# Making part of the routing one-hots on GpSimd instead of VectorE in a two-layer decoder block

## The chip, the cores and the metric

The kernel runs on one core of a Trainium2 chip. The metric is the device time of one execution in microseconds. A core has five engines that run side by side, each through its own list of instructions in order: TensorE (PE in the profile, its weight loads PEld), VectorE (DVE), ScalarE (ACT), GpSimd (POOL) and SyncE (SP, which here only issues transfers). Semaphores hold an instruction until what it needs is there.

## The reference: a two-layer decoder with an expert mixer in each layer

512 tokens of width 1024 pass two layers, the first with gated linear attention, the second with sliding-window attention. Each layer ends in a mixer over 16,384 single-neuron experts (PEER). For a token, 8 heads pick 16 experts each, by two keys of 128 values: expert number = first key x 128 + second key. Cut to what matters:

```
v1, i1 = top_k(s1, 16);  v2, i2 = top_k(s2, 16)       # per head, 128 keys each
cs, ci = top_k(v1[:, None] + v2[None, :], 16)
e = i1[ci // 16] * 128 + i2[ci % 16]                  # the 16 experts of a head
g = softmax(cs)
a = gelu(x . u_tab[e])
y = sum over heads and experts of g * a * v_tab[e]
```

## The kernel before: tiles, stages and what sets the order

Of the 512 tokens, 128 are done by *gathers*: GpSimd fetches the rows of the chosen experts from memory (line 717), and VectorE multiplies and adds them one expert at a time (lines 725 and 735). These are spread thinly over the whole dense stage of the layer.

The other 384 tokens are done *densely*: every expert is computed for every token, and a weight of zero takes out those that were not chosen. The function `dense` does it, once per layer. Its work has two parts.

The first part, called *pass 1* in the first layer and *pass 2* in the second, makes the routing weights. The 384 tokens are taken in 24 groups of 16. For a group, `routed(g)` works out the 128x128 matrix of weights of each token as a product of one-hot matrices: 128 (head, choice) pairs lie on the partitions, and for each token there is a matrix `o1` whose row has a one in the column of the pair's first key, and a matrix `o2` with a one at the second key. `og` is `o2` times the weight g, as a high and a low f16 half. Two matmuls per token, `o1` transposed times each half of `og`, sum over the pairs and give the token's 128x128 matrix. On VectorE a group takes one compare for `o2` (line 577), one compare for `o1` (line 579) and two products for `og` (line 582), each over 128 x 2048 f16 numbers. Compares are between `iop`, the numbers 0 to 127, each twice, and `i1T` or `i2T`, the transposed keys. TensorE then does 32 matmuls (line 590, the *routing matmuls*), ScalarE copies them out of PSUM (line 591), and a transfer writes them to a buffer in memory (`wd`, line 592).

Beside each group stands one call of `act(i)`, for one of 128 tiles of 128 experts: it loads the tile, splits it into a high half (ScalarE, line 243) and a low half (VectorE, line 244), and does 24 matmuls with the hidden state (line 605, the *activation matmuls*). 28 such tiles are done ahead.

The second part goes over all 128 tiles: it reads the weights back in slots (line 611), multiplies them with the activations (line 627), and accumulates the outputs with `stage2` (line 639).

The buffers that matter: `o1` has two buffers, `o2` and `og` have one each, `wt` two. The order of instructions on every engine is set by the framework's scheduler at build time, which goes by priorities and its own estimates of durations; a change of the code can move instructions on engines that it does not touch. The gathers have the lowest priority; each gather needs one of four row buffers.

The keys reach `dense` by `route_block`: three transposes on TensorE (line 545), and copies on ScalarE to `i1T`, `i2T` and the weights' halves `ghl` for each of three blocks of 128 tokens.

Of the kernel before, what the change touches and what calls it, by code (L numbers as in the profile page):

```python
# [10 lines left out]
F32 = mybir.dt.float32  # L11
# [5 lines left out]
ALU = mybir.AluOpType  # L17
# [3 lines left out]
P = 128  # L21
# [16 lines left out]
NBD = 3  # L38
TG = 16
# [9 lines left out]
def kernel(ctx, tc, x, c_col, pos, mod_w, mod_b, norm_g, w_in, w_gl, w_g2, b_g2, gla_ng, gla_wo,  # L49
                      kv_mod_w, kv_mod_b, kv_ng, kv_w, swa_wq, sinks, swa_wo, peer_wq, subk, peer_u, peer_v,  # L50
                      u_t, v_t, fin_g, out):
    nc = tc.nc

    const = ctx.enter_context(tc.tile_pool(name="const", bufs=1))
    mid = ctx.enter_context(tc.tile_pool(name="mid", bufs=1))
# [35 lines left out]
    iop = const.tile([P, NK, 2], F16, tag="iop", name="iop")  # L91
# [13 lines left out]
    def ps_tile(env, kind):  # L105
        pool, tag, bufs = env.psum[kind]
        if not isinstance(tag, str):
            pool, tag, bufs = tag[env.turn % len(tag)]
            env.turn += 1
        return pool.tile([P, 512], F32, tag=tag, name=f"ps_{kind}", bufs=bufs)  # L110
# [408 lines left out]
    def route_front(env, l, hT, rp):  # L519
        v16 = rp.tile([P, 16, TOPK], F32, tag="v16", name="v16")  # L520
        i16 = rp.tile([P, 16, TOPK], U32, tag="i16", name="i16")
        wpool, wtag, _, wbufs = env.w
        for ch in range(4):
            pq = ps_tile(env, "mm")
            for q in range(4):
                w = wpool.tile([P, KT, P], F32, tag=wtag, name="w", bufs=wbufs)
                nc.sync.dma_start(w, peer_wq[l, ch * 4 + q])
                for kt in range(KT):
                    nc.tensor.matmul(pq[:, ts(q, P)], w[:, kt, :], hT[:, kt, :], start=kt == 0, stop=kt == KT - 1)  # L529
            qq = env.big.tile([P, 512], F32, tag=env.qq, name="qq")  # L530
            nc.scalar.copy(qq, pq)
            psc = ps_tile(env, "sc")
            for q in range(4):
                nc.tensor.matmul(psc[:, ts(q, P)], qq[:, ts(q, P)], sk_sb[l][:, q % 2, :], start=True, stop=True)
            sc = env.tmp.tile([P, 512], F32, tag=env.t2k, name="scg", bufs=env.scb)
            nc.scalar.copy(sc, psc)
            topk16(rp, [(sc[:, ts(q, P)], v16[:, ch * 4 + q, :], i16[:, ch * 4 + q, :]) for q in range(4)], NK)
        return route(rp, v16, i16)

    def route_block(env, l, b, hT, rp):  # L540
        g, i1, i2 = route_front(env, l, hT, rp)
        e = b - 1
        pt = ps_tile(env, "tr")
        for q, t in enumerate((i1, i2, g.rearrange("p h k -> p (h k)"))):
            nc.tensor.transpose(pt[:, ts(q, P)], t, ident)
        nc.scalar.copy(i1T[e], pt[:, 0:P])
        nc.scalar.copy(i2T[e], pt[:, P:2 * P])
        gT = rp.tile([P, P], F32, tag="gT", name="gT")
        nc.scalar.mul(gT, pt[:, 2 * P:3 * P], GSC)
        nc.scalar.copy(ghl[e][:, 0, :], gT)  # L550
        nc.vector.tensor_tensor(ghl[e][:, 1, :], gT, ghl[e][:, 0, :], op=ALU.subtract)

    def dense(l, yps):
# [5 lines left out]
        with tc.tile_pool(name="dna", bufs=1, reuse_waits="tile") as da, \  # L559
# [5 lines left out]
            def routed(g):  # L565

                e, s16 = g // 8, ts(g % 8, TG)
                i1, i2, gh = (t.rearrange("p (u w) -> p u w", w=2) for t in (
                    i1T[e][:, s16], i2T[e][:, s16], ghl[e][:, 0, s16]))
                gl = ghl[e][:, 1, s16].rearrange("p (u w) -> p u w", w=2)  # L570
                codes = iop.unsqueeze(1).to_broadcast([P, TG // 2, NK, 2])

                def wide(t):
                    return t.unsqueeze(2).to_broadcast([P, TG // 2, NK, 2])

                o2 = do_.tile([P, TG // 2, NK, 2], F16, tag="o2", name="o2")
                nc.vector.tensor_tensor(o2, codes, wide(i2), op=ALU.is_equal)
                o1 = do_.tile([P, TG // 2, NK, 2], F16, tag="o1", name="o1", bufs=2)
                nc.vector.tensor_tensor(o1, codes, wide(i1), op=ALU.is_equal)
                og = do_.tile([P, 2, TG // 2, NK, 2], F16, tag="og", name="og")  # L580
                for n, gn in enumerate((gh, gl)):
                    nc.vector.tensor_tensor(og[:, n], o2, wide(gn), op=ALU.mult)
                wt = do_.tile([P, NK, TG], F32, tag="wt", name="wt", bufs=2)
                for q in range(4):
                    i = 4 * g + q
                    pm = yps.tile([P, 4, NK], F32, tag=banks[i % (3 if g < 16 else 6)], name="pm")
                    for t in range(4):
                        for n in range(2):
                            u, w = 2 * q + t // 2, t % 2
                            nc.tensor.matmul(pm[:, t, :], o1[:, u, :, w], og[:, n, u, :, w], start=n == 0, stop=n == 1)  # L590
                    nc.scalar.copy(wt[:, :, ts(q, 4)], pm.rearrange("p t i -> p i t"))
                nc.sync.dma_start(wd[ts(g, P), :], wt.rearrange("p i t -> p (i t)"))
# [266 lines left out]
    def swa_d(Y, yctx, mod, Ak, Bk, A, B, A4, B4, rbase):  # L859
        with ExitStack() as stack, tc.tile_pool(name="sd", bufs=1, reuse_waits="tile") as sp, \  # L860
# [50 lines left out]
            def finish(b):  # L911
                for ch in range(2):
                    w = stream_w(env, swa_wo[ch])
                    py = ps_tile(env, "mm")
                    for kt in range(KT):
                        nc.tensor.matmul(py, oT[b - 1][:, kt, :], w(kt), start=kt == 0, stop=kt == KT - 1)  # L916
                    gated_add(env, XD[b - 1], ch, py, gate[:, ts(ch, 512)])
                nc.sync.dma_start(xs[b], XD[b - 1])
                hT = h4k("hTd")
                env.psum["tr"] = env.psum["m0"]  # L920
                peer_h(env, b, XD[b - 1], A4, B4, hT)
                with prio(rbase):
                    route_block(renv, 1, b, hT, sr)
# [29 lines left out]
    i1T = [mid.tile([P, P], F16, tag=f"i1T{b}", name="i1T") for b in range(NBD)]  # L953
    i2T = [mid.tile([P, P], F16, tag=f"i2T{b}", name="i2T") for b in range(NBD)]
    ghl = [mid.tile([P, 2, P], F16, tag=f"ghl{b}", name="ghl") for b in range(NBD)]
    hH = mid.tile([P, KT, TD], F32R, tag="hH", name="hH")
    hL = mid.tile([P, KT, TD], F32R, tag="hL", name="hL")
    a0 = mid.tile([P, NH * TOPK], F32, tag="a0", name="a0")
# [34 lines left out]
    def fin0(env, pool, b, xt):  # L993
        nc.sync.dma_start(xs[b], xt)
        hT = pool.tile([P, KT, P], F32, tag="hTd", name="hTd", bufs=2)
        renv = Env()
        renv.psum, renv.tmp, renv.t2k, renv.big, renv.qq, renv.w = env.rpsum, pool, "rsc", pool, "qq", (pool, "w", 2, 3)
        renv.scb = 4
        if b == 0:
            ht = gather_front(env, pool, 0, xt, hT, m0[:, 40:48], cols["A2"], m0[:, 24:32])  # L1000
            with prio(R0):
                gs.append((ht, *gather_sel(renv, 0, hT, pool)))
        else:
            peer_h(env, b, xt, cols["A2"], m0[:, 24:32], hT)
            with prio(R0):
                route_block(renv, 0, b, hT, pool)
# [123 lines left out]
```

## Time and profile before

| what | value |
|---|---|
| median of 3 runs | 3281.14 us (3279.89 to 3283.94) |
| the profiled execution | 3281.36 us, of which the span is 3279.7 us |
| TensorE busy | 3087.9 us, 94% |
| VectorE busy | 2396.3 us, 73% |
| ScalarE busy | 1282.9 us, 39% |
| GpSimd busy | 610.3 us, 19% |
| first to last routing matmul, pass 1 | 578.1 to 721.8 us |
| first to last routing matmul, pass 2 | 2171.4 to 2302.9 us |

Matmuls are pipelined and overlap in the record, so TensorE's rate is read from starts, not from durations. VectorE's instructions overlap a little too: one starts before the one ahead of it has ended. A bracket behind a row of the timeline tells how long the engine was idle before it and what ended that. A granted clock of 1.00 is 2.4 GHz.

### The profile page before, as it was taken

The numbers are of one execution on the slowest core, as the hardware profiler recorded it, in microseconds if no ns is written. First come the engines' busy times: TensorE is split into PE (matmuls) and PEld (weight loads), VectorE is DVE, ScalarE is ACT, GpSimd is POOL, SyncE is SP. The second block draws the span as 40 slices with busy tenths as digits, with TensorE's granted clock in tenths as the row PEclk, the third lists the DMA queues.
The fourth block names the chain that finished last, engine by engine and source line by source line (L and its number), as shares of the span: only waits on it lengthen the run. The fifth ranks groups of instructions, "written<-read, shape, count | busy, mean of one in ns | idle before, by whom it ended". The sixth has DMA issues, their size and how long they took to land.

```text
span 3279.7 us, 45577 instructions
## 1 busy us (share of the span) xinstructions
PE 3087.9 (94%) x16858; PEld 2633.6 (80%) x16858; DVE 2396.3 (73%) x4699; ACT 1282.9 (39%) x1991; POOL 610.3 (19%) x542
## 2 busy tenths in 40 slices
PE   6999985999999999999997889899899999999998
PEld 4765675998889999999876446899789999999997
DVE  7754699989777777777655344999877777777776
ACT  3422322653333333333662344256333333333333
POOL 0000000005333333333000000000433232223230
PEclk9989998999999999999998989999999999999999
DMA  7666675789889898898744225658998888888874
GB/s 238 229 243 237 237 261 169 261 283 345 307 311 317 291 321 311 301 322 287 239 143 145 84 77 193 213 200 294 329 343 311 300 278 305 276 302 303 272 265 154
DMA packets 264888, 844.44 MB, mean 257 GB/s; under 512 B 27844, under 2 KB 77380, under 8 KB 258520
## 3 DMA queue, kind: packets, MB, share of 16 engines
q1 hardware_dynamic: 190936, 573.06, 49.4%
q0 software_dynamic: 73728, 268.47, 24.3%
q8 instruction: 132, 2.16, 0.3%
q14 instruction: 92, 0.75, 0.1%
HBM read 784.27 MB, written 57.16 MB: 257 GB/s over the span
## 4 chain that ended last, share of the span: by engine, by line
PE 81%; DVE 10%; DMA 5%; ACT 2%; issue 1%; SPq 0%; DVEq 0%; ACTq 0%
PE pa L605 32%; PE Y L639 30%; PE ps_mm L529 3%; PE pm L590 3%; PE ps_m L902 2%; DMA v<-in_v_t 1%; PE ps_mm L435 1%; PE ps_mm L260 1%; PE ps_mm L261 1%; PE ps_mm L259 1%; PE ps_mm L916 1%; DMA w<-in_gla_wo 1%; PE ps_po L808 1%; DMA w<-in_mod_w 1%; DVE s L446 1%
## 5 line engine op out<-in xcount | busy, mean ns | idle before, releaser
L717 POOL DMA_INDIRECT gu<-in_peer_u,ei x256 | 314.8, 1230 | 1991.3 <-DVE gu L725 1192.1
L244 DVE TENSOR_TENSOR XL<-u,XH 128x1024 fp32r<-128x1024 f32 x256 | 313.2, 1224 | 351.7 <-PE pa L605 197.4
L639 PE MATMUL Y<-XH,WH 128*128 128x512 f32 x1536 | 480.4, 393 | 9.8 <-ACT WH L243 9.8
L639 PE MATMUL Y<-XH,WL 128*128 128x512 f32 x1536 | 478.5, 393 | 4.1 <-DVE WL L244 4.1
L639 PE MATMUL Y<-XL,WH 128*128 128x512 f32 x1536 | 478.5, 392 | 0.2
L243 ACT CAST XH<-u 128x1024 fp32r<-128x1024 f32 x256 | 269.1, 1052 | 432.1 <-PE pa L605 359.2
L605 PE MATMUL pa<-hH,XH 128*128 128x384 f32 x2048 | 412.4, 341 | 2.2 <-ACT XH L243 1.6
L243 ACT CAST XH<-v 128x1024 fp32r<-128x1024 f32 x256 | 268.8, 1050 | 363.4 <-PE Y L639 312.2
L605 PE MATMUL pa<-hL,XH 128*128 128x384 f32 x2048 | 404.9, 336 | 0.0
L717 POOL DMA_INDIRECT gu<-in_peer_v,ei x256 | 290.9, 1136 | 608.6 <-DVE yg L735 567.4
L605 PE MATMUL pa<-hH,XL 128*128 128x384 f32 x2048 | 401.5, 335 | 2.2 <-DVE XL L244 2.2
L244 DVE TENSOR_TENSOR XL<-v,XH 128x1024 fp32r<-128x1024 f32 x256 | 313.0, 1223 | 109.9 <-ACT XH L243 106.2
L605 PEld LDWEIGHTS pa<-hH,XH 128*128 128x128 f32 x2048 | 365.1, 188 | 20.4 <-ACT XH L243 1.8
L605 PEld LDWEIGHTS pa<-hH,XL 128*128 128x128 f32 x2048 | 358.2, 188 | 3.2 <-DVE XL L244 2.9
L605 PEld LDWEIGHTS pa<-hL,XH 128*128 128x128 f32 x2048 | 358.8, 188 | 1.6 <-issue 0.8
L639 PEld LDWEIGHTS Y<-XH,WL 128*128 128x128 f32 x1536 | 289.0, 188 | 67.4 <-DVE WL L244 5.4
L639 PEld LDWEIGHTS Y<-XL,WH 128*128 128x128 f32 x1536 | 289.0, 189 | 64.4 <-DVE XL L244 1.1
L639 PEld LDWEIGHTS Y<-XH,WH 128*128 128x128 f32 x1536 | 286.3, 189 | 58.3 <-ACT WH L243 11.0
L735 DVE SCALAR_TENSOR_TENSOR yg<-gu,a,yg 128x1024 f32<-128x1024 f32 x254 | 325.0, 1279 | 1.4
L725 DVE SCALAR_TENSOR_TENSOR gu<-gu,htg 128x1024 f32<-128x1024 f32 x256 | 308.4, 1219 | 1.8 <-DMA gu<-in_peer_u,ei 1.7
L243 ACT CAST WH<-g 128x384 fp32r<-128x384 f32 x256 | 131.6, 514 | 383.4 <-DVE g L627 267.5
L529 PE MATMUL ps_mm<-hTd,w 128*128 128x128 f32 x1792 | 223.9, 279 | 10.1 <-DMA w<-in_peer_wq 8.2
(312 smaller groups left out, 3633.1 us busy)
## 6 DMA issues: line engine op xcount, KB each, us to landing
u<-in_u_t SPq DMA_DIRECT2D x256, 512.0 KB, 5.5
v<-in_v_t SPq DMA_DIRECT2D x256, 512.0 KB, 5.2
w<-in_peer_wq SPq DMA_DIRECT2D x128, 512.0 KB, 4.2
w<-in_mod_w SPq DMA_DIRECT2D x96, 512.0 KB, 5.0
wd<-wt SPq DMA_DIRECT2D x48, 1024.0 KB, 6.1
wg<-wd SPq DMA_DIRECT2D x192, 256.0 KB, 9.7
w<-in_gla_wo SPq DMA_DIRECT2D x32, 512.0 KB, 5.0
w<-in_swa_wo SPq DMA_DIRECT2D x32, 512.0 KB, 4.4
```

The lines of the kernel that those rows point to most:

```text
L243: nc.scalar.copy(H, src)
L244: eng.tensor_tensor(L, src, H.bitcast(F32), op=ALU.subtract)
L259: nc.tensor.matmul(out, ah, bh, start=kt == 0, stop=False)
L260: nc.tensor.matmul(out, ah, bl, start=False, stop=False)
L529: nc.tensor.matmul(pq[:, ts(q, P)], w[:, kt, :], hT[:, kt, :], start=kt == 0, stop=kt == KT - 1)
L590: nc.tensor.matmul(pm[:, t, :], o1[:, u, :, w], og[:, n, u, :, w], start=n == 0, stop=n == 1)
L605: nc.tensor.matmul(pa[:, :TD], uu[:, kt, :], hh[:, kt, :], start=n + kt == 0, stop=n == 2 and kt == KT - 1)
L639: nc.tensor.matmul(Y[b][h], a[:, ts(b, P)], vv[:, ts(h, 512)], start=i == 0 and a is WH and vv is VH, stop=i == NK - 1 and a is WL)
L717: nc.gpsimd.indirect_dma_start(out=u, out_offset=None, in_=table, in_offset=bass.IndirectOffsetOnAxis(ap=ei[:, i:i + 1], axis=0))
L725: nc.vector.scalar_tensor_tensor(u, u, 1.0, ht, op0=ALU.mult, op1=ALU.mult, accum_out=a[:, i:i + 1])
L735: nc.vector.scalar_tensor_tensor(y, u, a[:, i:i + 1], y, op0=ALU.mult, op1=ALU.add)
L902: nc.tensor.matmul(pqs[b], hTs[b][:, kt, :], w(kt), start=kt == 0, stop=kt == KT - 1)
```

## The change: three groups of four make the first-key one-hots on GpSimd

In groups 0, 1 and 2 of each four, the first-key matrix `o1` is no longer made by one VectorE compare of 2048 elements but by 16 GpSimd compares, one per token, each of 128 elements against one number per partition. That number comes from `i1F`, a f32 copy of the keys, which ScalarE makes beside `i1T`. Group 3 of each four stays as it was. The numbers written are the same.

```diff
--- before.py
+++ after.py
@@ -544,6 +544,7 @@
         for q, t in enumerate((i1, i2, g.rearrange("p h k -> p (h k)"))):
             nc.tensor.transpose(pt[:, ts(q, P)], t, ident)
         nc.scalar.copy(i1T[e], pt[:, 0:P])
+        nc.scalar.copy(i1F[e], pt[:, 0:P])
         nc.scalar.copy(i2T[e], pt[:, P:2 * P])
         gT = rp.tile([P, P], F32, tag="gT", name="gT")
         nc.scalar.mul(gT, pt[:, 2 * P:3 * P], GSC)
@@ -576,7 +577,12 @@
                 o2 = do_.tile([P, TG // 2, NK, 2], F16, tag="o2", name="o2")
                 nc.vector.tensor_tensor(o2, codes, wide(i2), op=ALU.is_equal)
                 o1 = do_.tile([P, TG // 2, NK, 2], F16, tag="o1", name="o1", bufs=2)
-                nc.vector.tensor_tensor(o1, codes, wide(i1), op=ALU.is_equal)
+                if g % 4 == 3:
+                    nc.vector.tensor_tensor(o1, codes, wide(i1), op=ALU.is_equal)
+                else:
+                    for t in range(TG):
+                        nc.gpsimd.tensor_scalar(o1[:, t // 2, :, t % 2], iop[:, :, 0], i1F[e][:, g % 8 * TG + t:g % 8 * TG + t + 1],
+                                                None, op0=ALU.is_equal)
                 og = do_.tile([P, 2, TG // 2, NK, 2], F16, tag="og", name="og")
                 for n, gn in enumerate((gh, gl)):
                     nc.vector.tensor_tensor(og[:, n], o2, wide(gn), op=ALU.mult)
@@ -953,6 +959,7 @@
     i1T = [mid.tile([P, P], F16, tag=f"i1T{b}", name="i1T") for b in range(NBD)]
     i2T = [mid.tile([P, P], F16, tag=f"i2T{b}", name="i2T") for b in range(NBD)]
     ghl = [mid.tile([P, 2, P], F16, tag=f"ghl{b}", name="ghl") for b in range(NBD)]
+    i1F = [mid.tile([P, P], F32, tag=f"i1F{b}", name="i1F") for b in range(NBD)]
     hH = mid.tile([P, KT, TD], F32R, tag="hH", name="hH")
     hL = mid.tile([P, KT, TD], F32R, tag="hL", name="hL")
     a0 = mid.tile([P, NH * TOPK], F32, tag="a0", name="a0")
```

On GpSimd, at the start of pass 1, the gathers of the first layer stood in one run (`gu` is the buffer of a fetched row, `in_peer_u` and `in_peer_v` the expert tables, `ei` the expert numbers).

```order
L330 MEMSET maskf 64x64
L717 DMA gu<-in_peer_u,ei 128x1024 x128
L717 DMA gu<-in_peer_v,ei 128x1024 x128
L717 DMA gu<-in_peer_u,ei 128x1024 x128
L717 DMA gu<-in_peer_v,ei 128x1024 x128
```

Now the first four gathers are followed by the compares, 16 to a group.

```order
L723 DMA gu_13873<-in_peer_u,ei_2529 128x1024
L723 DMA gu_13876<-in_peer_u,ei_2529 128x1024
L723 DMA gu_13879<-in_peer_u,ei_2529 128x1024
L723 DMA gu_13882<-in_peer_u,ei_2529 128x1024
L584 TENSOR_SCALAR o1_4376<-iop_94,i1F_171 128x128 x16
L584 TENSOR_SCALAR o1_4472<-iop_94,i1F_171 128x128 x16
L584 TENSOR_SCALAR o1_4568<-iop_94,i1F_171 128x128 x16
L584 TENSOR_SCALAR o1_4745<-iop_94,i1F_171 128x128 x16
```

Each layer has 18 such runs of 16, all ahead of its fifth gather.

On VectorE, some groups into pass 1, the order before was this for two and a half groups (`XL` is the low half of an expert tile).

```order
L579 TENSOR_TENSOR o1_4694<-iop_94,i1T_162 128x2048
L577 TENSOR_TENSOR o2_4692<-iop_94,i2T_165 128x2048
L244 TENSOR_TENSOR XL_4744<-u_4741,XH_4743 128x1024
L244 TENSOR_TENSOR XL_4825<-u_4822,XH_4824 128x1024
L582 TENSOR_TENSOR og_4696<-o2_4692,ghl_168 128x2048 x2
L579 TENSOR_TENSOR o1_4775<-iop_94,i1T_162 128x2048
L577 TENSOR_TENSOR o2_4773<-iop_94,i2T_165 128x2048
L244 TENSOR_TENSOR XL_4906<-u_4903,XH_4905 128x1024
L582 TENSOR_TENSOR og_4777<-o2_4773,ghl_168 128x2048 x2
```

Now, from a fourth group on, it is this.

```order
L581 TENSOR_TENSOR o1_5033<-iop_94,i1T_162 128x2048
L578 TENSOR_TENSOR o2_5031<-iop_94,i2T_165 128x2048
L244 TENSOR_TENSOR XL_5179<-u_5176,XH_5178 128x1024
L588 TENSOR_TENSOR og_5035<-o2_5031,ghl_168 128x2048 x2
L578 TENSOR_TENSOR o2_5112<-iop_94,i2T_166 128x2048
L244 TENSOR_TENSOR XL_5275<-u_5272,XH_5274 128x1024
L588 TENSOR_TENSOR og_5131<-o2_5112,ghl_169 128x2048 x2
L578 TENSOR_TENSOR o2_5208<-iop_94,i2T_166 128x2048
```

A group has five VectorE instructions before; after the change three groups in four have four of them, without the compare into `o1`.

On TensorE, at the end of pass 2, seven activation matmuls stood behind the last routing matmul before (`pa` is the activation's PSUM tile, `pm` the routing's, `Y` the output's).

```order
L590 LDWEIGHTS o1_19755
L590 MATMUL pm_19791<-og_19757,o1_19755 128x128
L605 MATMUL pa_19936<-hH_171,XL_19933 128x384 x7
L639 MATMUL Y_19978<-XH_19987,WH_19992 128x512
L639 MATMUL Y_19979<-XH_19987,WH_19992 128x512
```

Now more of them stand there.

```order
L596 LDWEIGHTS o1_20304
L596 MATMUL pm_20340<-og_20306,o1_20304 128x128
L611 MATMUL pa_20357<-hH_174,XH_20353 128x384 x3
L611 MATMUL pa_20357<-hL_175,XH_20353 128x384 x8
L611 MATMUL pa_20357<-hH_174,XL_20354 128x384 x8
L611 MATMUL pa_20389<-hH_174,XH_20385 128x384 x8
L611 MATMUL pa_20389<-hL_175,XH_20385 128x384 x8
L611 MATMUL pa_20389<-hH_174,XL_20386 128x384 x8
```

After these rows nine more of eight follow before the first `Y`: 115 activation matmuls in all, the end of one tile's and four whole tiles'. The scheduler had spread fewer of them between the groups.

## Rows read from the trace of the kernel before

**Rows 1.** The page's first line and its part 1: busy time by engine.

```profile
span 3279.7 us, 45577 instructions
PE 3087.9 (94%) x16858; PEld 2633.6 (80%) x16858; DVE 2396.3 (73%) x4699; ACT 1282.9 (39%) x1991; POOL 610.3 (19%) x542
```

**Rows 2.** Windows: stretch; length, busy PE, PEld, DVE, ACT, POOL; clock; DMA share, GB/s.

```profile
640.00:650.00 10.00, 10.00 (x102) 9.69 (x101) 9.38 (x9) 6.95 (x12) 0.00 (x0) 1.00 0.78 286
...
2240.00:2250.00 10.00, 10.00 (x97) 9.45 (x94) 10.00 (x10) 6.71 (x11) 0.00 (x0) 1.00 0.77 275
```

**Rows 3.** Timeline, one group of pass 1: start, length, engine, line, operation, idle before.

```profile
640.32 1.22 DVE L577 TENSOR_TENSOR o<-iop,i2T 128x2048 f16<-128x2048 f16 x1
...
640.93 2.02 PE L590 MATMUL pm<-og,o 128*128 128x128 f16 x32
...
642.76 1.64 PE L605 MATMUL pa<-hH,XH 128*128 128x384 f32 x8
642.98 2.36 DVE L582 TENSOR_TENSOR og<-o,ghl 128x2048 f16<-128x2048 f16 x2 [0.31 <-PE pm L590]
...
645.26 1.22 DVE L579 TENSOR_TENSOR o<-iop,i1T 128x2048 f16<-128x2048 f16 x1
...
645.62 1.55 PE L605 MATMUL pa<-hH,XL 128*128 128x384 f32 x8
...
646.40 1.22 DVE L577 TENSOR_TENSOR o<-iop,i2T 128x2048 f16<-128x2048 f16 x1
...
647.01 2.02 PE L590 MATMUL pm<-og,o 128*128 128x128 f16 x32
```

**Rows 4.** The routing matmuls' line in each pass: count, ns, first and last start.

```profile
L590 PE MATMUL pm<-og,o x768: 217/218/309, 578.1 to 721.8; 128*128 128x128 f16 x192
...
L590 PE MATMUL pm<-og,o x768: 217/218/238, 2171.4 to 2302.9; 128*128 128x128 f16 x192
```

**Rows 5.** Timeline, the end of pass 2.

```profile
2304.39 0.32 SPq L592 DMA_DIRECT2D wd<-wt  x1
...
2308.52 7.90 SPq L611 DMA_DIRECT2D wg<-wd  x13
2312.68 1.22 PE L639 MATMUL Y<-XH,WH 128*128 128x512 f32 x2 [8.25 <-ACT WH L243]
```

**Rows 6.** Instructions by line, 560 to 580 us: the copy beside the added one.

```profile
L546 ACT CAST i1T<-ps_tr 128x128 f16<-128x128 f32 x1 | 0.3, 265 | 5.1 <-PE ps_tr L545 5.1
```

**Rows 7.** Timeline of GpSimd alone, at the kernel's start.

```profile
2.45 1.52 POOL L92 IOTA iop<- 128x256 f16 x1
...
4.34 0.28 POOL L946 TENSOR_SCALAR_AFFINE_SELECT msk<-msk 128x128 f32<-128x128 f32 x1
4.59 0.28 POOL L948 TENSOR_SCALAR_AFFINE_SELECT msk<-msk 128x128 f32<-128x128 f32 x1
```

**Rows 8.** Timeline of GpSimd: the fifth gather of the first layer.

```profile
734.50 1.01 POOL L717 DMA_INDIRECT gu<-in_peer_u,ei  x1 [185.43 <-DVE gu L725]
```

**Rows 9.** Timeline, gathers beside VectorE's work, after pass 1.

```profile
751.64 0.55 DVE L244 TENSOR_TENSOR WL<-g,WH 128x384 fp32r<-128x384 f32 x1
...
752.78 1.23 DVE L244 TENSOR_TENSOR XL<-v,XH 128x1024 fp32r<-128x1024 f32 x1
752.83 1.99 POOL L717 DMA_INDIRECT gu<-in_peer_u,ei  x1 [0.30 <-DVE g L627]
...
753.92 1.22 DVE L725 SCALAR_TENSOR_TENSOR gu<-gu,htg 128x1024 f32<-128x1024 f32 x1
...
763.46 0.62 DVE L244 TENSOR_TENSOR WL<-g,WH 128x384 fp32r<-128x384 f32 x1 [0.24 <-ACT WH L243]
763.49 0.94 POOL L717 DMA_INDIRECT gu<-in_peer_u,ei  x1 [0.60 <-DVE gu L725]
```

**Rows 10.** Windows of 20 us with TensorE partly idle (columns as in rows 2).

```profile
440.00:460.00 20.00, 16.47 (x141) 15.71 (x139) 15.82 (x75) 2.50 (x7) 0.00 (x0) 1.00 0.86 298
...
1920.00:1940.00 20.00, 13.14 (x57) 7.26 (x57) 8.67 (x18) 8.26 (x25) 0.00 (x0) 0.74 0.00 0
```

## The prediction

> **What bounds the kernel now.** I began with the page's totals [rows 1]. The reader is to see that TensorE is busy for 94% of the span, VectorE for 73% and GpSimd for 19%: work moved from VectorE to GpSimd shortens the run only in a stretch where VectorE, not TensorE, is what ends last. The edited code runs in two short stretches, the first part of each layer's dense stage, which I call pass 1 and pass 2. Next I read the busy time per 10 us inside them [rows 2]: TensorE 10.00 and VectorE 9.38 of 10 in pass 1, 10.00 and 10.00 in pass 2, GpSimd 0.00 in both. So two engines are nearly full and the third is free.
>
> The timeline of one group in pass 1 says which of the two leads [rows 3]. Two successive second-key compares start at 640.32 and 646.40, a period of 6.08 us. TensorE runs the 32 routing matmuls from 640.93, the 24 activation matmuls from 642.76, and the next group's routing matmuls at 647.01: 6.08 us back to back. VectorE, at 642.98, has stood idle for 0.31 us waiting for those routing matmuls. Pass 1 is TensorE's, with VectorE 0.3 us behind. The length of the two passes I take from the first and last routing matmul [rows 4]: 578.1 to 721.8, 143.7 us, and 2171.4 to 2302.9. Pass 2 ends otherwise. The last block of weights is sent at 2304.39, read back from 2308.52, and TensorE's next matmul starts at 2312.68 after 8.25 us idle [rows 5]. From 2171.4 to that matmul is 141.3 us.
>
> **What the change does, with its costs.**
>
> *Removed.* VectorE loses 18 of 24 first-key compares in each pass. One VectorE instruction of this kind follows the other at 1.14 us (645.26 to 646.40 in rows 3), although each lasts 1.22. In pass 1 this saves nothing by itself, since TensorE's 6.08 us has no gap in it.
>
> *Moved.* The order pieces show how VectorE's list shrinks. Counted over its whole order, the changed kernel has between the first compare and the last product 103 two-tensor instructions in pass 1 (24 compares, 48 products, 6 remaining first-key compares, 25 low-half subtractions) and 93 in pass 2 (15 subtractions there). In pass 2 TensorE's activation matmuls are spread otherwise: 115 instead of 7 stand behind the last routing matmul. At eight in 1.39 us (645.62 to 647.01, rows 3) these are 20.0 us, enough to cover the 8.25 us of rows 5.
>
> *Added on ScalarE.* Six copies of a 128x128 block, each as its neighbour, 0.27 us [rows 6]. Only the last one in each pass stands before the first products: 0.5 us in all.
>
> *Added on GpSimd.* 18 x 16 = 288 compares of 128 elements per pass. The trace has none, so I bound one by the nearest GpSimd rows [rows 7]. Two operations that read and write 128x128 start 0.25 us apart (4.34 and 4.59). A generator of 128x256 f16 numbers, which like the new compares writes in two-byte numbers, took 1.52 us, 0.76 for half of it. I take 0.25, the row that has the same number of elements, one input and one output. GpSimd's queue hides none of this: the first four gathers stand ahead, and the fifth, which now stands behind the 288 compares, started only at 734.50 in the kernel before, after the pass [rows 8]. So the gathers are not made late as long as the pass stretches and they stretch with it.
>
> If the compares ran freely beside VectorE, 16 of them would be 4.0 us per group, and three groups in four 12 us of 24.3: hidden. The trace says that they do not run freely. Look at the gather that starts at 752.83 [rows 9]. VectorE's subtraction began at 752.78 and ends at 754.01. The gather ends at 754.82, 0.81 us behind that end, and lasts 1.99 us. The gather at 763.49 started 0.03 us behind a VectorE instruction and lasts 0.94 only, and the VectorE instruction took 0.62 us instead of the 0.55 of its like at 751.64. Whichever came first let the other wait. A gather reads one number per partition, and that short read is what waits. The next VectorE instruction after a waiting gather started on time (753.92), so such a short hold costs VectorE almost nothing; a compare holds longer.
>
> The Trainium skill ("SBUF — State Buffer", section "Who interferes with whom") states the rule: a VectorE instruction with two SBUF inputs and a GpSimd instruction that reads SBUF exclude each other, and the later one waits for the whole of the other. Every VectorE instruction of these passes has two SBUF inputs, so by the rule the two engines' times add instead of overlapping; the trace agrees for the gathers, with the 0.81 us above, and no row shows it for a 128-element compare.
>
> So I add the two engines. Pass 1: 103 x 1.14 = 117.4 and 288 x 0.25 = 72.0, together 189.4 against 143.7: +45.7. Pass 2: 93 x 1.14 = 106.0, plus 72.0, plus the 20.0 of matmuls behind the last routing matmul, 198.0 against 141.3: +56.7. Off goes what a handover hides: one VectorE instruction overlaps the next by 1.22 - 1.14 = 0.08 us, on 196 instructions -15.7. Plus 0.5 on ScalarE. Sum: +87.2. Added to the profiled execution's own 3281.36 us (its span is 3279.7 [rows 1]; the median of the three runs, 3281.14, lies within 0.3 us) this gives 3369 us.
>
> What is late next, where VectorE's 1.14 us goes: the routing matmuls wait for the first-key compares of their group on GpSimd. Behind them in TensorE's queue stand the activation matmuls, and behind those the copies and the subtractions that wait for the buffers. The second first-key buffer lets GpSimd work one group ahead, no more. The first two groups may be done before the pass starts, at best 32 x 0.25 = 8.0 us per pass, which I leave out because their buffer lies where earlier stages work.
>
> Bounds of the handover: if a compare that alternates with a VectorE instruction costs neither engine anything, only 288 - 103 and 288 - 93 compares are left to add: 117.4 + 46.3 - 143.7 = +20.0 and 106.0 + 48.8 + 20.0 - 141.3 = +33.5, 3335 in all. If a handover costs 0.1 us beyond it instead of saving 0.08, 3369 becomes 3404. If a compare costs 0.76, 576 x 0.51 = 294 more: 3662.
>
> TensorE's clock: its 6.08 us of work would stand in a period of 189.4 / 24 = 7.9 us, 77% busy. A stretch with 16.47 of 20 us busy was granted 1.00 (2.4 GHz throughout); one with 13.14 of 20 got 0.74, a mixture with the lower level, 1.2 GHz [rows 10]. At 0.77 the work would just fill 7.9 us, so I put nothing down.
>
> **Rivals.**
>
> *Free overlap.* The compares slip into the ends of VectorE's instructions as the gathers' reads do, without delay for either. For it: the instruction behind the waiting gather was on time (753.92). Against it: the 0.62 instead of 0.55 us, for a read of a single number. Then pass 1 stays at TensorE's pace and gains only its first compare, 1.1 us; pass 2 has its 8.25 us gap covered: 3272 us, faster. The point from which it decides is whether 16 compares of a group are through in 8.1 us (24.3 / 3) beside a busy VectorE.
>
> *Partial cover.* Exclusion holds, but the compares fall mostly into VectorE's waits for matmuls and casts, and the covered gap of pass 2 pays for the rest: anywhere between 3275 and 3330. Against it: pass 1 has only 0.31 us of wait per 6.08 [rows 3].
>
> *Slow compares.* A GpSimd compare with a number per partition and a stride of two is dearer than the nearest row. At twice the 0.25 the sum has 576 x 0.25 = 144 us more, 3513. For it: the 1.52 us row, which writes f16. Against it: that row writes a two-level pattern, the new compares a single one.
>
> The Trainium skill ("GPSIMD Engine Reference", section "Elementwise — side-by-side cycle accounting") gives GpSimd about 2.6 cycles an element at 1.2 GHz for two inputs, by which an estimate for 128 elements is 0.28 us and the dispatch; the sum by it would be some 17 us above mine, 3385, and no run here shows it for a compare.
>
> **How the numbers follow.** Exclusion at about 0.25 us a compare: 0.68, forecast 3369, its own range 3330 to 3410. Slow compares: 0.15, above 3410. Free overlap: 0.11, at 3272. Partial cover: 0.06. What a measurement of this kernel can tell from no change is 0.2%, 6.6 us. Free overlap's 3272 is faster by 9 us; of partial cover I count 0.03 as the same and 0.02 as slower and 0.01 as faster. So faster 0.12, same 0.03, slower 0.85. The range: 3290 to 3500. Below it lie free overlap and a little of partial cover, about 0.13; above it about half of the slow compares, 0.07.
>
> **What would show it.** In the changed profile the compares' starts should stand 0.25 us apart where VectorE waits, and more than 1 us apart where VectorE runs its two-tensor instructions; a VectorE compare beside them should last longer than 1.22 us or start late. The period of a group should rise from 6.08 to some 7.9 us in pass 1, with TensorE waiting for GpSimd's first-key block, and the 8.25 us gap of pass 2 should be gone. The prediction is wrong if the period stays near 6.1 us with the compares 0.25 us apart beside a busy VectorE (free overlap), or if the compares stand 0.5 us apart while VectorE is idle (slow compares).

## The result and the profile after: slower by 6.8%

The changed kernel takes 3505.8 us (median of 4 runs, 3500.9 to 3508.45) against 3281.64 us before (median of 4 runs, one more than in the table above): a ratio of 1.068, 95% interval 1.0666 to 1.0698. The profiled execution has a span of 3501.8 us, 222.1 us more than the 3279.7 of [rows 1]. The prediction had the sign, 87 us instead of 224, and a range that ended at 3500.

The page of the changed kernel: first line, part 1, the first line of part 4 (the chain that ended last), and from part 5 the new group and the routing matmuls, each with its busy time, its mean in ns, and the idle time ahead of it with what ended most of that.

```profile
span 3501.8 us, 46215 instructions
PE 3175.9 (91%) x16858; PEld 2684.9 (77%) x16858; DVE 2369.9 (68%) x4663; ACT 1292.3 (37%) x1997; POOL 1117.5 (32%) x1118
...
PE 68%; POOL 12%; DVE 9%; DMA 6%; ACT 2%; issue 2%; SPq 0%; DVEq 0%; ACTq 0%; POOLq 0%
...
L584 POOL TENSOR_SCALAR o<-iop,i1F 128x128 f16<-128x128 f16 x576 | 509.1, 933 | 363.2 <-DMA u<-in_u_t 322.1
...
L596 PE MATMUL pm<-og,o 128*128 128x128 f16 x1536 | 162.5, 251 | 145.1 <-POOL o L584 140.2
```

GpSimd has come onto the chain with 12% of the span, and a compare lasts 933 ns in the mean. In front of the routing matmuls TensorE stood idle for 145.1 us, 140.2 of them ended by a GpSimd compare. Where the time went is read from the routing matmuls' line in each pass, which answers to [rows 4].

```profile
L596 PE MATMUL pm<-og,o x768: 217/218/312, 573.4 to 822.3; 128*128 128x128 f16 x192
...
L596 PE MATMUL pm<-og,o x768: 217/288/330, 2270.5 to 2516.2; 128*128 128x128 f16 x192
```

Pass 1 is 248.9 us long instead of 143.7, pass 2 245.7 instead of 131.5. The time ahead of pass 1, that between the two passes and that behind the first output matmul of pass 2 moved by less than 5 us each. From the first routing matmul of pass 2 to the first output matmul it is 265.8 us (2270.5 to 2536.25, below) against 141.3.

The two passes as windows (columns as in rows 2):

```profile
573.40:822.30 248.90, 200.74 (x1320) 167.08 (x1320) 124.99 (x102) 91.01 (x144) 232.74 (x256) 0.81 0.44 162
2270.50:2516.20 245.70, 152.71 (x1134) 134.71 (x1134) 110.08 (x92) 75.21 (x125) 227.84 (x256) 0.78 0.39 141
```

VectorE, 9.4 of 10 busy before, is now half idle; GpSimd is busy for 232.74 of 248.90. 256 of the 288 compares are in each window: the other 32, of the first two groups, were done ahead of the pass. The granted clock has fallen to 0.81 and 0.78.

The timeline of one group of pass 1, answering to [rows 3]:

```profile
657.57 26.02 POOL L584 TENSOR_SCALAR o<-iop,i1F 128x128 f16<-128x128 f16 x31
...
664.08 0.29 PE L596 MATMUL pm<-og,o 128*128 128x128 f16 x2 [0.30 <-POOL o L584]
664.67 0.29 PE L596 MATMUL pm<-og,o 128*128 128x128 f16 x2 [0.30 <-POOL o L584]
665.25 0.39 PE L596 MATMUL pm<-og,o 128*128 128x128 f16 x2 [0.29 <-POOL o L584]
...
670.07 2.91 PE L611 MATMUL pa<-hH,XH 128*128 128x384 f32 x8
...
670.35 2.63 DVE L588 TENSOR_TENSOR og<-o,ghl 128x2048 f16<-128x2048 f16 x2 [7.41 <-PE pm L596]
...
676.79 1.16 PE L596 MATMUL pm<-og,o 128*128 128x128 f16 x14
```

The reader is to see three things. TensorE takes most of the 32 routing matmuls in pairs, one token at a time, each pair 0.585 us behind the last and released by a GpSimd compare; before, all 32 took 2.02 us. VectorE stands idle for 7.41 us because its product buffer waits for those matmuls. And the eight activation matmuls behind them last 2.91 us instead of 1.64: after the waits they run at the lower level of the clock, 1.2 GHz (0.50 granted from 670 to 673 us). All 24 take 6.72 us (670.07 to 676.79) where they took 4.25 before (642.76 to 647.01 in rows 3). GpSimd meanwhile works on without a break, 31 compares from 657.57 to 683.59.

At the end of pass 2 the gap of [rows 5] is gone, as foreseen: the last weights are written and read back while activation matmuls run. The first output matmul has no wait in front of it.

```profile
2517.36 0.32 SPq L598 DMA_DIRECT2D wd<-wt  x1
...
2523.69 1.40 SPq L617 DMA_DIRECT2D wg<-wd  x3
...
2536.25 0.63 PE L645 MATMUL Y<-XH,WH 128*128 128x512 f32 x2
```

### The profile page after: what moved, and what is told of

It reads as the page before. It is cut to its first block, busy times and chain, and to the rows that moved or that the text cites. A ratio compares the mean times of both kernels' runs of the same rounds, so it can differ in the third digit from the quotient of the medians.

```text
span 3501.8 us, 46215 instructions
## 1 busy us (share of the span) xinstructions
PE 3175.9 (91%) x16858; PEld 2684.9 (77%) x16858; DVE 2369.9 (68%) x4663; ACT 1292.3 (37%) x1997; POOL 1117.5 (32%) x1118
## 4 chain that ended last, share of the span: by engine, by line
PE 68%; POOL 12%; DVE 9%; DMA 6%; ACT 2%; issue 2%; SPq 0%; DVEq 0%; ACTq 0%; POOLq 0%
PE Y L645 26%; PE pa L611 26%; POOL o L584 12%; PE ps_mm L529 3%; PE ps_m L908 2%; PE ps_mm L435 1%; DMA w<-in_mod_w 1%; PE ps_mm L922 1%; DMA v<-in_v_t 1%; DVE gacc L131 1%; DMA u<-in_u_t 1%; PE ps_mm L260 1%; PE pm L596 1%; PE ps_po L814 1%; DMA w<-in_gla_wo 1%
## 5 line engine op out<-in xcount | busy, mean ns | idle before, releaser
L584 POOL TENSOR_SCALAR o<-iop,i1F 128x128 f16<-128x128 f16 x576 | 509.1, 933 | 363.2 <-DMA u<-in_u_t 322.1
L611 PE MATMUL pa<-hH,XH 128*128 128x384 f32 x2048 | 434.6, 354 | 3.8 <-ACT g L613 2.2
L611 PE MATMUL pa<-hL,XH 128*128 128x384 f32 x2048 | 417.6, 343 | 0.0
L611 PEld LDWEIGHTS pa<-hH,XH 128*128 128x128 f32 x2048 | 384.2, 198 | 22.4 <-ACT g L613 3.4
L611 PEld LDWEIGHTS pa<-hL,XH 128*128 128x128 f32 x2048 | 372.7, 195 | 1.6 <-issue 0.8
L596 PE MATMUL pm<-og,o 128*128 128x128 f16 x1536 | 162.5, 251 | 145.1 <-POOL o L584 140.2
```

Source lines behind the costliest of these rows:

```text
L584: nc.gpsimd.tensor_scalar(o1[:, t // 2, :, t % 2], iop[:, :, 0], i1F[e][:, g % 8 * TG + t:g % 8 * TG + t + 1], None, op0=ALU.is_equal)
L611: nc.tensor.matmul(pa[:, :TD], uu[:, kt, :], hh[:, kt, :], start=n + kt == 0, stop=n == 2 and kt == KT - 1)
```

## Experiments: what a compare costs, and who waits for whom

**What a compare costs alone.** Eight forms of one small GpSimd instruction at the kernel's start, into a tile that nobody reads.

```diff
+    for _ in range(6):
+        nc.gpsimd.tensor_scalar(p16[:, :, 0], iop[:, :, 0], ones1[:, 0:1], None, op0=ALU.is_equal)
+        nc.gpsimd.tensor_scalar(pc[:, 0:NK], ic[:, 0:NK], ones1[:, 0:1], None, op0=ALU.is_equal)
+        nc.gpsimd.tensor_scalar(p32[:, 0:NK], pf[:, 0:NK], ones1[:, 0:1], None, op0=ALU.is_equal)
+        nc.gpsimd.tensor_scalar(p16[:, 0:64, 0], iop[:, 0:64, 0], ones1[:, 0:1], None, op0=ALU.is_equal)
+        nc.gpsimd.tensor_scalar(pc, ic, ones1[:, 0:1], None, op0=ALU.is_equal)
+        nc.gpsimd.tensor_scalar(p16[:, :, 0], iop[:, :, 0], 1.0, None, op0=ALU.is_equal)
...
```

> The kernel before, with eight forms of one small GpSimd instruction, six times each, put at its start into a tile that nobody reads. It asks what a compare costs by itself and what of it is dear. Compare-price theory: the form used in the change (f16, every second element, number per partition) stands near 0.59 us while VectorE is idle or has one input, and one of its parts explains it: if the stride, the contiguous form is near 0.3; if f16, the f32 form is near 0.3; if the pointer, the form with a constant is near 0.3; if it is per instruction, 64, 128 and 256 elements cost nearly the same; if it is per element, 64 costs about half and 256 about double. Exclusion-only theory: the form costs 0.25 to 0.3 alone and only reaches 0.59 beside VectorE. Whole time: 3281 to 3320 by all of them, since these 48 instructions stand ahead of the first mask only.

Lines 99 to 104 of that kernel, one row each: count, then ns as least/median/most. The least is that beside an idle VectorE.

```profile
L99 POOL TENSOR_SCALAR p<-iop,ones x6: 638/966/1244, 4.2 to 38.1; 128x128 f16<-128x128 f16 x6
...
L100 POOL TENSOR_SCALAR p<-iop,ones x6: 594/602/832, 5.4 to 39.3; 128x128 f16<-128x128 f16 x6
...
L101 POOL TENSOR_SCALAR p<-pf,ones x6: 595/600/609, 4.8 to 11.4; 128x128 f32<-128x128 f32 x6
...
L102 POOL TENSOR_SCALAR p<-iop,ones x6: 457/509/1393, 6.6 to 40.2; 128x64 f16<-128x64 f16 x6
...
L103 POOL TENSOR_SCALAR p<-iop,ones x6: 931/1260/1777, 7.2 to 41.4; 128x256 f16<-128x256 f16 x6
...
L104 POOL TENSOR_SCALAR p<-iop x6: 560/660/1106, 8.7 to 43.1; 128x128 f16<-128x128 f16 x6
```

The form of the change lasts 0.638 us alone. Neither the stride (0.594 without), nor f16 (0.595 in f32), nor the number per partition (0.560 with a constant) is what makes it dear: the stride adds 0.04 us and the number per partition 0.08. The two forms not shown, at their least: a multiplication in the form of the change takes 0.647 us, and a subtraction of two contiguous inputs 0.427, less than a compare with one. Contiguous, 128 elements take 0.594 and 256 take 0.931: by these two, 2.6 ns an element and 0.26 us for the instruction, which comes to 75 us for the 288 of a pass. My nearest row, 0.28 us for the same 128x128 elements [rows 7], was of another operation and no guide to this one. The whole run, one execution, took 3295.04 us, inside the expected span. The Trainium skill ("GPSIMD Engine Reference", section "Engine selection") calls one-input elementwise work on GpSimd roughly line rate; here 2.6 ns an element is some three cycles of the 1.2 GHz that the page gives the engine, and the measurement decides.

**Compares that nobody waits for.** The kernel before, with compares beside VectorE's unchanged work.

```diff
                 nc.vector.tensor_tensor(o1, codes, wide(i1), op=ALU.is_equal)
+                if g % 4 != 3 and g:
+                    src = ahead[:, g - 1, 0:NK]
+                    nc.gpsimd.tensor_scalar(spare[:, :, 0], src, ones1[:, 0:1], None, op0=ALU.is_equal)
+                    for t in range(1, TG):
+                        nc.gpsimd.tensor_scalar(spare[:, :, t % 2], iop[:, :, 0], ones1[:, 0:1], None, op0=ALU.is_equal)
```

> The kernel before, all first-key compares on VectorE as they were, and beside them 272 GpSimd compares per pass (16 for each of 17 groups, paced by the activation of the tile before) that write a tile nobody reads. No instruction waits for them. Exclusion theory: each of pass 1's 119 VectorE instructions lets one compare in between and starts about 0.5 us later, so pass 1 grows by 119 x 0.5 = 60 us or somewhat less, pass 2 by as much or less, in all 3340 to 3400 us, and VectorE's two-input instructions stand 1.6 us apart instead of 1.14. Price-only theory (a compare is slow, but the engines overlap): VectorE's instructions stay 1.14 apart and the time is 3275 to 3295.

The time was 3358.51 us, ratio 1.024 (1.0203 to 1.0268), within what the exclusion theory gave, but not for its reason. Pass 1 did not grow by 60 us but by 0.4 (579.7 to 723.8, 144.1 us against 143.7), pass 2 by 5 (2213.7 to 2350.0, 136.3 against 131.5). Its timeline on VectorE and GpSimd:

```profile
638.87 7.00 POOL L584 TENSOR_SCALAR spare<-iop,ones 128x128 f16<-128x128 f16 x3
...
641.86 1.21 DVE L579 TENSOR_TENSOR o<-iop,i1T 128x2048 f16<-128x2048 f16 x1
642.99 1.31 DVE L577 TENSOR_TENSOR o<-iop,i2T 128x2048 f16<-128x2048 f16 x1
644.23 1.21 DVE L244 TENSOR_TENSOR XL<-u,XH 128x1024 fp32r<-128x1024 f32 x1
645.36 2.44 DVE L587 TENSOR_TENSOR og<-o,ghl 128x2048 f16<-128x2048 f16 x2
```

Three compares take 7.00 us: 2.33 us each, the length of two VectorE instructions, where one takes 0.585 alone. VectorE gives up very little: every second instruction lasts 1.31 instead of 1.21 us and starts 1.24 instead of 1.13 behind the last. So they do exclude each other, but the loser is GpSimd. Most of the extra 77 us of the whole run came later: GpSimd ran behind, the gathers queued up behind the spare compares (the fifth started at 787.41 instead of 734.50), and VectorE waited for its data. The waits from 700 to 900 us (engine and line, what it waited for, us in total, times, longest):

```profile
DVE gu L730 <- DMA gu<-in_peer_u,ei: 41.8, 4, 40.1
```

The second layer has such a wait of 29.2 us. The two waits and the 5 us of pass 2 are 74 of the 77.

**The same with writes only.** Six number generators that read nothing stand in place of 15 of the 16 compares.

```diff
-                    for t in range(1, TG):
-                        nc.gpsimd.tensor_scalar(spare[:, :, t % 2], iop[:, :, 0], ones1[:, 0:1], None, op0=ALU.is_equal)
+                    for t in range(6):
+                        nc.gpsimd.iota(spare, [[1, NK], [0, 2]], base=0, channel_multiplier=0, ...)
```

> The same kernel and pace as the one with spare compares, but behind the one paced compare of a group stand six GpSimd instructions that only write (number generators of 256 f16, 1.52 us each alone, 9.1 us a group, as much GpSimd time as 16 compares at 0.59). Exclusion of reads: VectorE goes on at 1.14 us apart, 3278 to 3300. Exclusion of any GpSimd access: VectorE loses 1.5 us for each, 102 per pass, 3400 us and more. Price-only theory: 3275 to 3295.

```profile
642.51 9.36 POOL L584 IOTA spare<- 128x256 f16 x6
644.61 1.22 DVE L579 TENSOR_TENSOR o<-iop,i1T 128x2048 f16<-128x2048 f16 x1
645.74 1.22 DVE L577 TENSOR_TENSOR o<-iop,i2T 128x2048 f16<-128x2048 f16 x1
646.35 2.02 PE L596 MATMUL pm<-og,o 128*128 128x128 f16 x32
646.88 1.22 DVE L244 TENSOR_TENSOR XL<-u,XH 128x1024 fp32r<-128x1024 f32 x1
```

Six in 9.36 us, 1.56 each, hardly more than alone (1.52, rows 7), and VectorE's instructions keep their 1.22 us and their starts. These generators, which only write, do not collide with VectorE. The Trainium skill says so too ("SBUF — State Buffer", section "Who interferes with whom": a VectorE instruction with two SBUF inputs contends with a GpSimd instruction that reads SBUF, not with one that only writes). The page's rule that whichever of the two starts first keeps the other waiting for the whole instruction (section "SBUF: two separate sides") the traces bear out for GpSimd alone; VectorE lost 0.1 us for a compare. The whole time, 3387.44 us (ratio 1.033, 1.0295 to 1.0365), is no test of it and lies above the 3278 to 3300 of the theory that the rows bear out: the longest waits for a gather's data are 57.6 us in the first layer and 50.5 in the second, together as much as the run lost (105), since the generators too kept the gathers behind them. Pass 1 (144.5 us) and pass 2 (131.9) stayed as they were.

```profile
DVE gu L731 <- DMA gu<-in_peer_u,ei: 59.1, 3, 57.6
```

**No replacement at all.** The changed kernel without the GpSimd compares.

```diff
-                    for t in range(TG):
-                        nc.gpsimd.tensor_scalar(o1[:, t // 2, :, t % 2], iop[:, :, 0], i1F[e][...], None, op0=ALU.is_equal)
+                    o1 = fixed.unsqueeze(1).to_broadcast([P, TG // 2, NK, 2])
```

> The changed kernel with the GpSimd compares left out: in three groups of four the first-key one-hots are a constant tile of zeros, so the routing weights of these groups are zero. It shows what taking the work off VectorE buys when its replacement costs nothing. By the sum of the prediction TensorE's 6.08 us a group stays in pass 1 and the 8.25 us gap at the end of pass 2 is covered: 3272 us (3266 to 3278). If VectorE had been the bound of pass 2 more than I read, down to 3262. If the new order of the other engines is itself the loss, above 3290.

3271.36 us, ratio 0.996 (0.9947 to 0.9978). This is the most that the move can bring, 10 us, as the prediction had it. The first output matmul of pass 2 comes at 2303.90 instead of 2312.68 and without a wait: the covered gap is most of it. The rest has a reason too: in the kernel before, the first output matmuls behind the 8.25 us of waiting ran at the lower level of the clock (0.50 granted from 2312.68 to 2315.41), the first two in 1.22 us [rows 5], where they take 0.63 here.

```profile
2303.90 0.63 PE L643 MATMUL Y<-XH,WH 128*128 128x512 f32 x2
```

**One group in four on GpSimd.**

```diff
-                if g % 4 == 3:
+                if g % 4:
```

> The changed kernel with GpSimd making the first-key one-hots of one group in four instead of three. Starved-GpSimd theory (VectorE is hardly delayed, a compare takes 0.59 us while VectorE is idle and two VectorE instructions, 2.3 us, while it is busy; who waits is the routing matmuls): 16 compares get through only in part while VectorE works on, then VectorE runs dry and the rest go at 0.59, some 3 us for every fourth group, 18 per pass, less some cover at the end of pass 2: 3295 to 3335. Added-engines theory of the prediction with the price corrected (113 x 1.14 + 96 x 0.585 = 185 us against 143.7, less handover): 3340 to 3365. Price-only theory (9.4 us in every 24.3 are hidden): 3268 to 3283.

3355.84 us, ratio 1.021 (1.0165 to 1.0246). This lies in the range that the added engines gave with the price corrected, and my starved estimate was short. But it is no adding of two busy engines. Pass 1 is 181.6 us (579.0 to 760.6), 6.3 us more for every fourth group. The timeline shows why:

```profile
628.33 17.26 POOL L584 TENSOR_SCALAR o<-iop,i1F 128x128 f16<-128x128 f16 x16 [14.59 <-PE pm L596]
...
641.56 0.29 PE L596 MATMUL pm<-og,o 128*128 128x128 f16 x2 [0.29 <-POOL o L584]
642.14 0.39 PE L596 MATMUL pm<-og,o 128*128 128x128 f16 x2 [0.30 <-POOL o L584]
...
646.08 2.36 DVE L588 TENSOR_TENSOR og<-o,ghl 128x2048 f16<-128x2048 f16 x2 [5.67 <-PE pm L596]
```

GpSimd stood idle for 14.59 us for a free first-key buffer, then made its 16 compares in 17.26 us: eight in the first 12.6 us, while VectorE had work, then one per 0.585 us while VectorE stood idle and TensorE and ScalarE waited for each pair. Averages hide this: 9.4 us in every 24.3 would fit, but the two buffers let GpSimd begin only two groups ahead, while VectorE is busy.

**Only the first two groups of each pass.**

```diff
-                if g % 4 == 3:
+                if g >= 2:
```

> The changed kernel with GpSimd making only the one-hots of groups 0 and 1 of each pass, which have their own buffers and can be made before the pass starts, while VectorE still sorts for the last block. Starved-GpSimd theory: the 32 compares lie ahead of the pass, nobody waits, VectorE saves two compares per pass: 3272 to 3281. If the buffer is free only when the pass starts: 16 compares at 0.59 to 2.3 us stand before the first matmul and the next group, 3285 to 3310.

3284.51 us, ratio 1.0003 (0.9988 to 1.0018): no change that can be told, where I expected 3272 to 3281. No routing matmul waited for GpSimd there, so the compares were done ahead; the four VectorE instructions saved brought nothing that the measurement shows. Here the order left only 19 activation matmuls behind the last routing matmul, and the gap at the end of pass 2 stayed:

```profile
2314.97 1.22 PE L645 MATMUL Y<-XH,WH 128*128 128x512 f32 x2 [8.39 <-ACT WH L243]
```

**Twice as many compares of half the size.**

```diff
-                        nc.gpsimd.tensor_scalar(o1[:, t // 2, :, t % 2], iop[:, :, 0], ...
+                        for k in (0, 64):
+                            nc.gpsimd.tensor_scalar(o1[:, t // 2, k:k + 64, t % 2], iop[:, k:k + 64, 0], ...
```

> The changed kernel with each GpSimd compare split in two of 64 elements, same result, 576 instead of 288 per pass. Alone a pair costs 2 x 0.37 = 0.74 us from start to start against 0.585. Starved-GpSimd theory, the wait being per instruction: the price adds 288 x 0.16 = 45 us per pass and the waits beside VectorE (some 80 us of the 249 of pass 1) grow by up to as much again: 3640 to 3760. If the wait goes by elements, or if the pass is GpSimd's own price alone: 3580 to 3610. If TensorE's lower clock is what lengthens the pass: hardly more than 3505, below 3560.

3644.14 us, ratio 1.109 (1.1038 to 1.1138), at the lower edge of the per-instruction range, in part by luck, as the rows show. Pass 1 is 324.0 us (575.6 to 899.6), 75 more than in the changed kernel, so the pass follows GpSimd's work and not the clock alone, by which it was to stay below 3560. The row of its compares in pass 1, and two pairs of routing matmuls from a stretch in which VectorE is idle:

```profile
L585 POOL TENSOR_SCALAR o<-iop,i1F 128x64 f16<-128x64 f16 x525 | 313.1, 644 | 3.1 <-PE pm L597 3.1
...
656.42 0.29 PE L597 MATMUL pm<-og,o 128*128 128x128 f16 x2 [0.53 <-POOL o L585]
657.24 0.29 PE L597 MATMUL pm<-og,o 128*128 128x128 f16 x2 [0.53 <-POOL o L585]
```

Two halves take 0.82 us from start to start, not the 0.74 I had put down: 525 x 0.41 = 215 us of compares against 150, most of the 75. Their median is 0.462 us, that of one alone 0.457 at the least, so 525 x (0.644 - 0.462) = 96 us were waits beside VectorE, against 83 for half as many compares. The waits hardly grew with the number of compares, against the theory: they go by the number of VectorE instructions, 102 in both.

**A constant instead of a number per partition.** First in the kernel with the spare compares:

```diff
-                        nc.gpsimd.tensor_scalar(spare[:, :, t % 2], iop[:, :, 0], ones1[:, 0:1], None, op0=ALU.is_equal)
+                        nc.gpsimd.tensor_scalar(spare[:, :, t % 2], iop[:, :, 0], 1.0, None, op0=ALU.is_equal)
```

> The kernel before with the spare compares that nobody reads, as measured before, but comparing with a constant instead of a number per partition (all but the first of a group). There a compare took 2.33 us beside a busy VectorE, two of its instructions. If one of the two is the read of the number per partition: 1.17 us, one VectorE instruction per compare, and each VectorE instruction 0.1 us longer instead of every second one. If a compare waits twice for another reason (read and write, say): 2.33 us as before.

```profile
643.59 2.27 POOL L582 TENSOR_SCALAR spare<-ahead,ones 128x128 f16<-128x128 f32 x1
...
645.94 8.52 POOL L584 TENSOR_SCALAR spare<-iop 128x128 f16<-128x128 f16 x7
...
650.26 1.30 DVE L579 TENSOR_TENSOR o<-iop,i1T 128x2048 f16<-128x2048 f16 x1
651.49 1.30 DVE L577 TENSOR_TENSOR o<-iop,i2T 128x2048 f16<-128x2048 f16 x1
652.72 1.30 DVE L244 TENSOR_TENSOR XL<-u,XH 128x1024 fp32r<-128x1024 f32 x1
```

Seven compares in 8.52 us: 1.22 each, one VectorE instruction instead of two, and every VectorE instruction is now 1.30 us long, 1.23 apart. The first row is the one compare of a group that kept its number per partition: 2.27 us in the same stretch. The second wait belongs to the read of the number per partition. (One execution, 3322.77 us.)

Then in the changed kernel itself:

```diff
-  nc.gpsimd.tensor_scalar(o1[:, t // 2, :, t % 2], iop[:, :, 0], i1F[e][...], None, op0=ALU.is_equal)
+  nc.gpsimd.tensor_scalar(o1[:, t // 2, :, t % 2], iop[:, :, 0], float(g % 8 * TG + t), None, op0=ALU.is_equal)
```

> The changed kernel with each GpSimd compare against a constant instead of the token's key, so that the first-key one-hots of three groups in four have the wrong column. Everything waits as in the changed kernel. Starved-GpSimd theory with two waits per compare, one of them for the number per partition: alone a compare stands 0.51 us apart instead of 0.585, 256 x 0.075 = 19 us less per pass, and of the some 80 us of waits beside VectorE in pass 1 (65 in pass 2) half goes: in all about 110 us less, 3380 to 3410. If a compare waits once whatever it reads: 38 us less, 3460 to 3475. If the pass hangs on TensorE's lower clock: 3490 to 3510.

3463.13 us, ratio 1.056 (1.0535 to 1.0575): 43 us less than the changed kernel, where I expected about 110. Pass 1 is 227.9 us (571.2 to 799.1). One half of the expectation failed: in a row, the compares with a constant stand 0.64 us apart, not 0.51, as the matmul pairs that they release show.

```profile
645.14 0.29 PE L595 MATMUL pm<-og,o 128*128 128x128 f16 x2 [0.35 <-POOL o L584]
645.78 0.29 PE L595 MATMUL pm<-og,o 128*128 128x128 f16 x2 [0.35 <-POOL o L584]
646.42 0.29 PE L595 MATMUL pm<-og,o 128*128 128x128 f16 x2 [0.35 <-POOL o L584]
```

With 256 x 0.64 = 164 us for the compares and 11 of waiting for a buffer, 53 us are left of the 227.9, against 248.9 - 150 - 12 = 87 in the changed kernel. The whole time alone would fit the rival of a single wait (3460 to 3475), but that had the compares cheaper and the waits unchanged, and here the row of compares is dearer. So the waits did fall by some 40%, and a dearer row of compares gave part of it back. Why a shorter instruction stands farther apart in a row is open.

**The covered gap alone.** Nothing on GpSimd; the version without compares had shown what paid, the activation matmuls behind the last routing matmul.

```diff
-NA = 28
+NA = 30
```

> The kernel before, nothing on GpSimd, but 30 instead of 28 expert tiles done ahead, so that two whole tiles (48 matmuls, 8.4 us) stand behind the last routing matmul of pass 2. It tries the one part of the change that paid (the covered 8.25 us at the end of pass 2) without GpSimd. Cover theory: 3272 to 3276. If the gain of the version without compares came from VectorE instead: 3279 to 3284. If the later start of the second part costs in pass 1 what it covers in pass 2: 3281 to 3290.

3271.81 us, ratio 0.9974 (0.9961 to 0.9987), the median of 12 runs: 0.3% faster than the kernel before, with an interval that excludes 1, and just below the 3272 to 3276 of the cover theory. The wait in front of pass 2's first output matmul has shrunk from 8.25 to 0.26 us, and the granted clock behind it is 1.00 (2309.15 to 2311.00).

```profile
2309.15 0.73 PE L639 MATMUL Y<-XH,WH 128*128 128x512 f32 x2 [0.26 <-ACT WH L243]
```

## Why the prediction was right in sign and wrong in size

*What bounds the kernel, and what is removed: right.* Without VectorE's compares and without a replacement the kernel gains 10 us, against the 3272 us worked out for free overlap.

*The price of a compare: this is the step that failed.* The sum took "0.25, the row that has the same number of elements, one input and one output". A compare stands 0.585 us apart alone. The 288 a pass are 168.5 us instead of 72.0, 193 more in both passes. With this alone the sum gives 3562. The range's upper end had been set at half of the slow-compare rival, whose 3513 for a price of 0.50 comes near the measured time; that is luck, since at the price that was measured the same sum gives 3562. The rival was right that a compare is dear, and the sign that the prediction named for it (0.5 us apart while VectorE is idle) is what the profile shows. Its grounds were not: f16 adds nothing, the stride 0.04 us and the number per partition 0.08. Of the 0.594 us of a contiguous compare 0.26 falls on the instruction and 0.34 on its 128 elements, each as much or more than the 0.25 taken for the whole. A chance of 0.15 was too low for a price taken from another operation.

*The first two groups ahead: priced, then left out.* The reason given, buffers that lie where earlier stages work, did not hold: they were done before both passes (in the first layer from 545.3 us on; 256 compares in each window), 32 x 0.585 = 18.7 us a pass. That brings 3562 to 3524.

*Adding the two engines: nearly right as a sum, wrong as a picture.* I had VectorE and GpSimd take turns at equal cost. In fact VectorE is hardly delayed, by 0.1 us a handover, and a compare beside it waits for up to two of its instructions. That the sum with the right price ends within 20 us of the measured time is two errors against each other: it has 208 us of VectorE's time where 148 of waits were, and nothing for the 41 us that GpSimd waited for a free buffer. In the changed kernel the compares of the two passes show it:

```profile
L584 POOL TENSOR_SCALAR o<-iop,i1F 128x128 f16<-128x128 f16 x256 | 232.7, 959 | 11.9 <-PE pm L596 11.9
...
L584 POOL TENSOR_SCALAR o<-iop,i1F 128x128 f16<-128x128 f16 x256 | 227.8, 939 | 29.1 <-PE pm L596 28.0 <-ACT wt L597 1.1
```

Pass 1: 256 x 0.585 = 150 us of compares, 256 x (0.959 - 0.636) = 83 of waits beside VectorE (0.636 is the median of all compares and stands for one without a wait), 12 of waiting for a buffer, together 245 of the 248.9. The 83 are 0.8 us for each of the 103 VectorE instructions where the sum had 1.14 less 0.08. Pass 2: 150, 65 and 29, 244 of 245.7. That the two passes follow GpSimd is shown by the split compares; that part of the waits is the number per partition, by the constant ones.

*The clock: wrong, and of no proven weight.* I put nothing down at 77% busy; it fell to 0.81 and 0.78, at a TensorE that waits for several us in each group and then works in a block. GpSimd is busy or waiting for VectorE in all but 12 and 29 us of the passes, so by this reckoning what the clock can have cost is within these; it was not tried apart.

*Free overlap and partial cover:* ruled out by the 2.33 us of a spare compare, where the first needed 16 in 8.1 us, and by the passes' lengths. *The gap of pass 2:* covered, as foreseen, and worth its 8 us, with some 1.5 more for the matmuls behind it that ran at the lower clock, only where nothing else is lost.

## What to carry to other kernels

Price an operation that moves to another engine by that operation in that form, with a few spare copies in an idle stretch, before it is weighed in a sum: here the nearest row was wrong by a factor of more than two. Where one large instruction becomes many small ones, count what each costs before its first element. Where the receiving engine reads the same memory as a busy one, count its instructions' waits one by one and look at how far its buffers let it run ahead, since an average that fits can still stall every group. And look at what a change of order brings by the way: covering one round trip through memory by two more tiles gave all that this move could have given.

## What the runs showed of the hardware that was not expected

- A GpSimd compare costs about 0.26 us and 2.6 ns for each element of a partition: 0.594 us for 128 and 0.931 for 256; 0.595 for 128 in f32, and 0.638 with a stride of two.
- Beside a busy VectorE with two SBUF inputs, a GpSimd compare takes 2.33 us with a number per partition and 1.22 with a constant; VectorE loses about 0.1 us for each.
- GpSimd's number generators, which only write, run beside VectorE hardly disturbed: 1.56 us against 1.52 alone.
- After 8.25 us of idling TensorE ran its next six matmuls at 1.2 GHz (0.50 granted from 2312.68 to 2315.41 in the kernel before), so this gap cost more than its length.
